# Macaron encoder layer on one Trainium2 core: inputs transposed by numpy, first blocks on undivided inputs, twelve blocks begun, a hand-set order of the end

## The chip, the cores and the metric

The kernel runs on one core of a Trainium2 chip. The core has five engines that each work through their own instructions in order: PE (matrix products into PSUM), DVE (VectorE), ACT (ScalarE), POOL (GpSimd) and SP (here it only issues DMAs). The metric is the device time of one execution in microseconds (us), lower is better; a program is run several times and the median counts. A profile is the record of one more execution.

## The reference, cut to what matters

Two independent token streams, x_prompt and x_sample, 512 tokens x 1024 channels each, float32, go through one layer and a last norm:

```
rms_norm(x, g) = x * rsqrt(mean(x*x, axis=-1) + 1e-6) * g
swiglu(x)      = (silu(x @ w_gate) * (x @ w_up)) @ w_down      # 1024 -> 2816 -> 1024
x = x + 0.5 * swiglu(rms_norm(x, ffn1_norm))                   # FFN1
x = x + mix(rms_norm(x, mix_norm))                             # attention and mLSTM, side by side
x = x + 0.5 * swiglu(rms_norm(x, ffn2_norm))                   # FFN2
y = rms_norm(x, final_norm)
```

The mean in rms_norm goes over the channels of one token, so 1/rms is one number for each token; it can be multiplied into x before a matrix product or into the product's result.

## The kernel before, in words

**Numbers.** Every float32 operand of a product is split into a high part (ACT copies it to the rounded type) and a low part (DVE subtracts the high part). A product of 128 x 128 by 128 x 512 is then three PE instructions: high by high, high by low, low by high. `w_pair` (L241) splits weights, `put` (L227) right operands.

**An FFN's first half.** A scheme of seven products in place of eight works on gate and up weights, the lower and upper half of the 1024 channels, and the two streams at once. Its seven right operands `xc` are B11 and B21 (lower and upper half of stream 0), B22 (upper half of stream 1) and the sums and differences T1 to T4. For one block of 128 of the 2816 columns (22 blocks) each of the seven is 4 x 3 = 12 PE instructions. `gu_first` (L286) does B11 and B21, which need stream 0 and the gate weights alone; its results are v1 (after B11) and silu(g0) (after B21). `gu_rest` (L301) does the other five. A block can be *begun* ahead: `begin` (L395) does B11 and B21 and parks v1 and silu(g0) in DRAM (`kept`), from where `resume` loads them. `rest` (L404) then goes through the blocks in the order `ORDER` (L368): resumed and fresh ones take turns while there are resumed ones. Before, AHEAD = 7 blocks are begun in both FFNs, so ORDER is 0, 7, 1, 8, ... 6, 13, 14, ... 21. Weights come through four buffers `wr` of 512 KB and, split, four buffers `w8`.

**An FFN's second half.** `ffn_down` (L449) multiplies by w_down in 28 steps (four groups of blocks by seven products, L533), whose operands were written to DRAM (`rbuf`) and are loaded again (`rt`). `flush_` (L541) adds each result from PSUM into the residual streams `xs` and calls `done(s, h, b)` when the block of tokens b, half h of the channels, stream s is complete.

**Opening.** `load_x` (L1148) loads raw tokens, 128 tokens x 1024 channels at a time, 512 KB each. `norm_x` (L1188) takes their sums of squares on DVE (L1195), 1/rms with `rstd_cols` (L151: a first guess from the bits of the number and three Newton steps, 12 small DVE operations) and multiplies it into the rows (L1201 on ACT, L1203 on DVE). `turn` (L1152) turns them with PE transposes (L1155) so that channels lie on partitions, `first_x` (L1215) multiplies with the norm's weights `g1` and splits (L1218 on ACT, L1219 on DVE). `park_x` (L1223) writes stream 0 to DRAM (`xnbuf`); `sums_of` (L1244) loads it again for the sums T1 to T4. Seven blocks are begun in between. `g1` is gathered by a DMA on POOL's queue (L125).

**End.** `done2` (L1346) takes the squares of a finished 128 x 512 piece on ACT (L1160), multiplies with `final_norm` (L1349, on POOL or DVE), and when a pair of token blocks is complete calculates 1/rms, multiplies it in (L1361 DVE, L1363 ACT) and stores 128 tokens x 1024 channels, 512 KB (L1364, SP's queue).

**What sets the order.** A list scheduler of the framework orders the instructions of each engine by readiness and priority. `shifted` moves a priority, `pin` (`keep_in_program_order`) keeps marked instructions in the order of the program. Nearly all DMAs are issued on SP's queue, in order. PSUM has pools of 3 (`MM`), 1 (`PO`), 2 (`PS`) and 2 (`PT`) banks.

Of the kernel before, what the change touches and what calls it, by code (L numbers as in the profile page):

```python
# [16 lines left out]
P = 128  # L17
# [9 lines left out]
def encoder(ctx, tc, I, outs):  # L27
# [97 lines left out]
    nc.gpsimd.dma_start(g1, I["ffn1_norm"][0].rearrange("(k p) -> p k", p=P))  # L125
# [25 lines left out]
    def rstd_cols(v, width, n):  # L151


        def t_(dt=F32):
            w = max(width, 4)
            return spool.tile([P, w], dt, tag=f"rs{w}", bufs=5, name=nm("rs"))[:, 0:width]
        V = nc.vector
        a = t_()
        V.tensor_scalar(a, v, 1.0 / n, EPS, op0=ALU.mult, op1=ALU.add)
        b = t_(I32)  # L160
        V.tensor_scalar(b, a.bitcast(I32), 1, None, op0=ALU.logical_shift_right)
        y_ = t_(I32)
        V.tensor_scalar(y_, b, -1.0, 1597463007.0, op0=ALU.mult, op1=ALU.add)
        y = y_.bitcast(F32)
        for _ in range(3):
            t = t_()
            V.scalar_tensor_tensor(t, y, -0.5, y, op0=ALU.mult, op1=ALU.mult)
            V.tensor_tensor(t, t, a, op=ALU.mult)
            r = t_()
            V.scalar_tensor_tensor(r, t, 1.5, y, op0=ALU.add, op1=ALU.mult)  # L170
            y = r
        return y

    def col_sums(acc, bs=(0, 1, 2, 3)):
# [4 lines left out]
        nc.vector.tensor_reduce(c, p[:, bs[0] * P:(bs[-1] + 1) * P].rearrange("p (b d) -> p b d", d=P), axis=AX.X,  # L179
                                op=ALU.add)  # L180
        return c
# [184 lines left out]
    AHEAD = 7  # L366

    ORDER = [j for p in zip(range(AHEAD), range(AHEAD, NF)) for j in p] + list(range(2 * AHEAD, NF))  # L368

    class Up:  # L370


        def __init__(self, xc, wg, wu, rb):
            self.xc, self.rb = xc, rb
            self.v = wg, wu
# [13 lines left out]
            r.junk = [r.o.rows[1][:, i] for i in range(2)]  # L389
            r.lone, r.last = lone, fa  # L390
# [13 lines left out]
        def rest(self, raw, at=None, hook=None):  # L404
            ring = self.ring
# [43 lines left out]
    def ffn_down(wd, rb, ring, tail, xres, done, at_step, hook):  # L449
# [19 lines left out]
        def load_raw(fp, i):  # L469
# [3 lines left out]
            fb = ORDER[2 * fp + i]  # L473
# [67 lines left out]
        def flush_(i, d, p):  # L541
# [3 lines left out]
            if last and m == T1:  # L545
                acc = xs[1][:, DH + d]
            if i < 7 and m in (B11, T2_, T1):
                nc.scalar.activation(acc, p, AF.Copy, scale=0.5)
            else:
                V_.scalar_tensor_tensor(acc, p, 0.5, acc, op0=ALU.mult, op1=ALU.add)  # L550
# [13 lines left out]
            elif m == T1:  # L564
                done(1, 1, d)
# [575 lines left out]
    raws = [A([P, 4, D], F32, "raw") for _ in range(2)]  # L1141
    xc = [None] * 7
    up = Up(xc, I["ffn1_w_gate"], I["ffn1_w_up"], rbuf[0])
    xins = [I[n][0] for n in ("x_prompt", "x_sample")]

    kept = [[dpool.tile([P, S], F32, name=f"kept{j}_{i}") for i in range(2)] for j in range(AHEAD)]

    def load_x(s):  # L1148
        for b in range(4):
            nc.sync.dma_start(raws[s][:, b, :], xins[s][b * P:(b + 1) * P, :])  # L1150

    def turn(s, k, banks):  # L1152
        p = banks[k % len(banks)]()
        for b in range(4):
            nc.tensor.transpose(p[:, b * P:(b + 1) * P], raws[s][:, b, k * P:(k + 1) * P], ident)  # L1155
        return p
# [31 lines left out]
    def norm_x(s):  # L1188

        sq = [spool.tile([P, 4], F32, tag="cs4", bufs=4, name=nm("cs4")) for _ in range(2)]  # L1190
        junk = up.ring.junk
        for b in range(4):
            for i in range(2):
                x_ = raws[s][:, b, i * S:(i + 1) * S]
                pin(V_.scalar_tensor_tensor(junk[i], x_, 1.0, x_, op0=ALU.mult, op1=ALU.mult,  # L1195
                                            accum_out=sq[i][:, b:b + 1]))
        pin(V_.tensor_tensor(sq[0], sq[0], sq[1], op=ALU.add))
        rs = rstd_cols(sq[0], 4, D)
        for b in range(4):
            if b % 2:  # L1200
                pin(nc.scalar.activation(raws[s][:, b, :], raws[s][:, b, :], AF.Copy, scale=rs[:, b:b + 1]))  # L1201
            else:
                pin(V_.tensor_scalar(raws[s][:, b, :], raws[s][:, b, :], rs[:, b:b + 1], None, op0=ALU.mult))  # L1203

    load_x(0)
    raw0 = up.fetch(0, (0,))
    load_x(1)
    raw1 = [up.fetch(j, (0,))[0] for j in (1, 2)]
    norm_x(0)
    W = [gu_left_a(raw0[0], pin)]  # L1210
    xc[B11], xc[B21] = xc_tile(), xc_tile()
    every = [PS, PT, PS, PT, MM, MM, PO]
    ps0 = {}

    def first_x(k):  # L1215
        t, kk, g = xc[B11 if k < HK_ else B21], k % HK_, g1[:, k:k + 1]
        p = ps0[k] = turn(0, k, every)
        nc.scalar.activation(t[:, 0, kk, :], p, AF.Copy, scale=g)  # L1218
        V_.scalar_tensor_tensor(t[:, 1, kk, :], p, g, f(t[:, 0, kk, :]), op0=ALU.mult, op1=ALU.subtract)  # L1219

    parked = []

    def park_x(k):  # L1223
        if k % 2 == 0:
            parked.append(up.ring.x())
        nc.scalar.activation(parked[-1][:, k % 2], ps0.pop(k), AF.Copy, scale=g1[:, k:k + 1])
        if k % 2:
            nc.sync.dma_start(xnbuf[:, k - 1:k + 1, :], parked[-1])

    for k in range(KD - 1):  # L1230
        first_x(k)
    park_x(0)
    first_x(KD - 1)
    W.append(gu_left_a(raw1[0], pin))
    up.begin(0, W[0])
    for k in range(1, KD):
        park_x(k)
    up.begin(1, W[1])
    norm_x(1)
    W.append(gu_left_a(raw1[1], pin))  # L1240
    raw0 += up.fetch(0, (1,))
    for i in (T2_, T1, T3, B22, T4):
        xc[i] = xc_tile()
# [10 lines left out]
    for k in (0, 2):  # L1254
        W.append(up.left(3 + k))
        sums_of(k, lambda kk, bank: turn(1, kk, [bank]), g1)
        W.append(up.left(4 + k))
        if k == 0:
            up.begin(2, W[2])
    for j in (3, 4, 5, 6):  # L1260
        up.begin(j, W[j])

# [5 lines left out]
    def done1(s, h, b):  # L1268
# [53 lines left out]
    up = Up(xc, I["ffn2_w_gate"], I["ffn2_w_up"], rbuf[1])  # L1322
# [23 lines left out]
    def done2(s, h, b):  # L1346
        x_ = xs[s][:, h * 4 + b, :]
        square(x_, ssq3[s][:, h, b:b + 1])
        (V_ if (s, h) == (1, 0) else G_).tensor_tensor(x_, x_, fn[h], op=ALU.mult)  # L1349
        if s == 0 and h == 1 and b == 3:  # L1350
            n = slice(0, 4)
        elif s == 1 and h == 0 and b % 2:
            n = slice(b - 1, b + 1)
        else:
            return
        r = row_scale(ssq3[s], n)
        for i in range(n.start, n.stop):
            v = xs[s].rearrange("p (h b) c -> p h b c", h=2)[:, :, i, :]
            r_ = r[:, i - n.start:i - n.start + 1]
            if s and i == 3:  # L1360
# [71 lines left out]
```

## Time and profile before

| | us |
|---|---|
| median of 3 runs (lowest, highest) | 2118.5 (2116.89, 2118.99) |
| the profiled execution | 2116.6 |
| its span (first to last record) | 2114.8 |
| PE busy in it | 2068.3 |
| first product of the FFN starts | 20.33 |
| first product of FFN1's second half starts | 450.10 |
| last product of the kernel starts (9 instructions, 2.20 us) | 2098.16 |

Times in the profile count from the start of the span. In a row of the timeline the columns are start, duration, engine, line, operation, what is written and read, shape, how many (x), and in brackets how long the engine had been idle before and what ended that. L12 is line 12 of the kernel that the row belongs to. Matmul durations overlap, so the distance from one start to the next is the time that one takes.

### The profile page before, as it was taken

What the parts mean: (1) busy time and instruction counts of PE and PEld (TensorE: products, weight loads), DVE (VectorE), ACT (ScalarE), POOL (GpSimd) and SP (SyncE); (2) the same over time, 40 slices, a digit from 0 to 9 for tenths busy, and PEclk for the clock granted to TensorE, in tenths of its full rate; (3) what the DMA queues carried; (4) which work ended last, traced back from release to release, by engine and by line L of the source; (5) the groups of instructions that cost most, each with busy time, mean ns of one, the idle gap of its engine ahead of it and who ended that gap; (6) DMA issues with size and microseconds to landing.
All of it is one profiled execution on the core that took longest, in us unless ns stands there. A gap on an engine that the chain in (4) does not pass through costs nothing.

```text
span 2114.8 us, 26230 instructions
## 1 busy us (share of the span) xinstructions
PE 2068.3 (98%) x9472; PEld 1692.4 (80%) x9472; DVE 1558.7 (74%) x2583; ACT 940.2 (44%) x1565; POOL 103.2 (5%) x110
## 2 busy tenths in 40 slices
PE   6999999999999999999999999999999999999997
PEld 5888888888888777878887787788888888888885
DVE  7888787776796896574649855754887877786696
ACT  6443443442225566463436555544544434343223
POOL 1000000001000110000101101010000000000002
PEclk9999999999999999999999999999999999999999
DMA  7464653489764222232341222354546545379763
GB/s 268 151 223 166 209 179 140 148 325 379 266 229 140 76 75 77 82 119 83 111 160 59 72 97 72 130 164 163 171 163 205 198 160 179 130 277 396 264 212 123
DMA packets 137425, 361.76 MB, mean 171 GB/s; under 512 B 13296, under 2 KB 13312, under 8 KB 136272
## 3 DMA queue, kind: packets, MB, share of 16 engines
q1 hardware_dynamic: 136704, 358.83, 48.6%
q0 software_dynamic: 592, 1.27, 0.2%
q8 instruction: 74, 1.21, 0.2%
q14 instruction: 55, 0.45, 0.1%
HBM read 255.15 MB, written 104.89 MB: 170 GB/s over the span
## 4 chain that ended last, share of the span: by engine, by line
PE 86%; DVE 7%; ACT 3%; DMA 2%; issue 1%; SPq 0%; POOL 0%; DVEq 0%; ACTq 0%; POOLq 0%
PE pss L283 17%; PE mm L686 14%; PE pst L283 11%; PE mm L283 10%; PE mm L533 7%; PE mm L670 4%; PE pst L533 4%; PE pss L533 4%; PE mm L1115 3%; PE pso L533 2%; PE pso L942 2%; PE pso L670 1%; PE pso L1071 1%; PE pss L914 1%; PE pss L1022 1%; PE pso L1115 1%
## 5 line engine op out<-in xcount | busy, mean ns | idle before, releaser
L283 PE MATMUL pss<-xc,w 128*128 128x512 f32 x1584 | 379.1, 389 | 0.0
L283 PEld LDWEIGHTS pss<-xc,w 128*128 128x128 f32 x1584 | 297.2, 188 | 62.0 <-DVE t L313 0.2
L686 PE MATMUL mm<-xh,w 128*128 128x512 f32 x896 | 294.1, 397 | 0.0
L283 PE MATMUL mm<-xc,w 128*128 128x512 f32 x1056 | 254.7, 391 | 2.9 <-ACT f L292 2.2
L242 ACT ACTIVATE w<-wr 128x1024 fp32r<-128x1024 f32 x132 | 139.7, 1060 | 235.3 <-PE pst L283 142.0
L283 PEld LDWEIGHTS mm<-xc,w 128*128 128x128 f32 x1056 | 196.7, 188 | 47.8 <-ACT f L292 6.3
L205 DVE TENSOR_TENSOR w<-wr,w 128x1024 fp32r<-128x1024 f32 (+1 forms) x112 | 136.6, 1221 | 114.1 <-ACT w L204 108.9
L243 DVE TENSOR_TENSOR w<-wr,w 128x1024 fp32r<-128x1024 f32 x132 | 161.1, 1222 | 80.2 <-ACT w L242 79.9
L686 PEld LDWEIGHTS mm<-xh,w 128*128 128x128 f32 x896 | 167.8, 189 | 32.4
L533 PE MATMUL mm<-w,rt 128*128 128x512 f32 x792 | 185.6, 389 | 0.9 <-DMA rt<-rbuf 0.9
L686 PE MATMUL mm<-xl,w 128*128 128x512 f32 x448 | 177.5, 396 | 0.0
L533 PEld LDWEIGHTS mm<-w,rt 128*128 128x128 f32 x792 | 148.4, 188 | 32.2 <-DMA rt<-rbuf 1.5
L204 ACT ACTIVATE w<-wr 128x1024 fp32r<-128x1024 f32 (+1 forms) x112 | 114.6, 1030 | 113.5 <-PE pso L1115 35.0
L283 PE MATMUL pst<-xc,w 128*128 128x512 f32 x528 | 127.1, 389 | 0.0
L283 PE MATMUL pst<-xc,f 128*128 128x512 f32 x528 | 127.0, 389 | 0.0
L283 PEld LDWEIGHTS pst<-xc,w 128*128 128x128 f32 x528 | 99.0, 188 | 20.8 <-ACT t L316 0.3
L283 PEld LDWEIGHTS pst<-xc,f 128*128 128x128 f32 x528 | 99.1, 188 | 20.6
L590 ACT ACTIVATE w<-t 128x512 fp32r<-128x512 f32 x82 | 51.6, 632 | 121.8 <-PE pst L533 63.6
L590 ACT ACTIVATE w<-wr 128x512 fp32r<-128x512 f32 x72 | 44.6, 631 | 129.8 <-PE pso L533 65.7
L686 PEld LDWEIGHTS mm<-xl,w 128*128 128x128 f32 x448 | 84.6, 189 | 16.2
L533 PE MATMUL pss<-w,rt 128*128 128x512 f32 x396 | 95.2, 390 | 1.3 <-ACT w L590 1.3
L533 PE MATMUL pst<-w,rt 128*128 128x512 f32 x396 | 94.3, 389 | 0.0
(323 smaller groups left out, 3497.8 us busy)
## 6 DMA issues: line engine op xcount, KB each, us to landing
rt<-rbuf SPq DMA_DIRECT2D x154, 512.0 KB, 6.2
rbuf<-t SPq DMA_DIRECT2D x72, 512.0 KB, 3.2
wr<-in_ffn_w_gate_dram SPq DMA_DIRECT2D x56, 512.0 KB, 4.2
wr<-in_w_in_cols_dram SPq DMA_DIRECT2D x56, 512.0 KB, 3.5
wr<-in_ffn_w_up_dram SPq DMA_DIRECT2D x44, 512.0 KB, 3.5
rbuf<-f SPq DMA_DIRECT2D x30, 512.0 KB, 3.2
rbuf<-tab SPq DMA_DIRECT2D x30, 512.0 KB, 3.6
wr<-in_ffn_w_down_dram SPq DMA_DIRECT2D x48, 256.0 KB, 7.6
```

Source lines behind the costliest of these rows:

```text
L204: pin(nc.scalar.activation(hi, raw, AF.Copy))
L205: pin(lo_eng.tensor_tensor(lo, raw, f(hi), op=ALU.subtract))
L242: pin(nc.scalar.activation(t[:, 0], src, AF.Copy))
L243: pin(V_.tensor_tensor(t[:, 1], src, f(t[:, 0]), op=ALU.subtract))
L283: nc.tensor.matmul(p, a[:, k, :], xt[:, b, k, :], start=(first and k == 0 and i == 0), stop=(k == HK_ - 1 and i == 2), skip_group_check=True)
L533: nc.tensor.matmul(p, r[:, b, d * P:(d + 1) * P], u[:, a, :], start=(first and q == 0 and k == 0), stop=(q == len(us) - 1 and k == 2), ski ...
L590: nc.scalar.activation(hi, src, AF.Copy)
L670: nc.tensor.matmul(p[b][:, :N], a[:, k, bs], w_[:, kl, :], start=(k == 0 and i == 0), stop=(k == KD - 1 and i == 2))
L686: nc.tensor.matmul(p, a[:, k, :], b, start=(k == 0 and i == 0), stop=(k == n - 1 and i == 2))
L914: nc.tensor.matmul(p, qT[:, h, b * P:(b + 1) * P], kv[:, hk * 2 + j, :], start=(j == 0), stop=(j == 1))
L942: nc.tensor.matmul(po, Vst[:, kv_, hk, :], w, start=(kv_ == 0 and i == 0), stop=(kv_ == 3 and i == 1))
L1115: nc.tensor.matmul(p[b], a[:, k, bs], w_[:, k - k0, :], start=(k == 0 and i == 0), stop=(k == KD - 1 and i == 2))
```

## The change

- numpy, ahead of the launch, transposes both inputs to channels on partitions (`x_prompt_t`, `x_sample_t`) and lays `ffn1_norm` out as 128 x 8; `g1` is loaded on SP's queue. `turn`, `norm_x`, `first_x` and `park_x` with their 64 PE transposes go.
- The first six blocks are begun on stream 0 times `g1` without 1/rms. The squares go to ACT (128 x 1024 at a time), their sums to DVE, the sum over partitions and the spreading of 1/rms along the tokens to PE transposes (`col_sums`, `bcast_psum`, 16 in all); `raw_end` multiplies 1/rms (R) into v1 and g0 on DVE before the Silu.
- Both streams are then multiplied by `g1` and R in place (`normed`), split anew, and blocks 6 to 11 begun on them: 12 blocks in FFN1, 7 still in FFN2. With 12, ORDER is 0, 12, 1, 13, ... 9, 21, 10, 11. The sums T1 to T4 are made on chip from 128 x 2048 operands.
- 1/rms is one Newton step and one of higher order: 11 small DVE operations for 12, everywhere.
- The end: `ends2` takes over the last product's results. Products with `final_norm` go to `e16` and `e5`, the mean square of half a row with eps is kept in `half_ms`, 1/rms of a pair starts from one fused operation (`last_scale`), the last piece is taken from PSUM in two halves of 256, stores of stream 1 are 256 KB each and two of them are issued by ACT. Stream 0's scaling and stores are spread between stream 1's squares on ACT.

The core of the diff:

```diff
-    nc.gpsimd.dma_start(g1, I["ffn1_norm"][0].rearrange("(k p) -> p k", p=P))
+    nc.sync.dma_start(g1, I["ffn1_norm"])
...
-        for _ in range(3):
-            t = t_()
-            V.scalar_tensor_tensor(t, y, -0.5, y, op0=ALU.mult, op1=ALU.mult)
-            V.tensor_tensor(t, t, a, op=ALU.mult)
-            r = t_()
-            V.scalar_tensor_tensor(r, t, 1.5, y, op0=ALU.add, op1=ALU.mult)
-            y = r
-        return y
+        t = t_()
+        pin(V.scalar_tensor_tensor(t, y, -0.5, y, op0=ALU.mult, op1=ALU.mult))
+        pin(V.tensor_tensor(t, t, a, op=ALU.mult))
+        pin(V.scalar_tensor_tensor(t, t, 1.5, y, op0=ALU.add, op1=ALU.mult))
+        y, t, p, q = t, y, b.bitcast(F32), t_()
+        pin(V.tensor_tensor(t, y, y, op=ALU.mult))
+        pin(V.tensor_tensor(t, t, a, op=ALU.mult))
+        pin(V.tensor_scalar(p, t, 0.375, -1.25, op0=ALU.mult, op1=ALU.add))
+        pin(V.tensor_tensor(p, p, t, op=ALU.mult))
+        pin(V.scalar_tensor_tensor(q, p, 1.875, y, op0=ALU.add, op1=ALU.mult))
+        return q
...
-    AHEAD = 7
+    RAW, AHEAD = 6, (12, 7)
+    def order_of(ahead):
+        return [j for p in zip(range(ahead), range(ahead, NF)) for j in p] + (
+            list(range(2 * ahead, NF)) or list(range(NF - ahead, ahead)))
...
+    load_half(0, 0)
+    load_x(0, 0, 1)
+    load_x(0, 1, 2)
+    load_x(0, 2, 4)
+    load_half(1, 0)
+    load_half(0, 1)
+    load_x(0, 4, 6)
+    load_x(0, 6, 8)
+    load_half(1, 1)
+    raw2 = up.fetch(2, (0,))
+    for k in range(0, KD, 2):
+        load_x(1, k, k + 2)
...
+    def split_x(k):
+        t, kk, g, x = xr[k // HK_], k % HK_, g1[:, k:k + 1], x_t[0][:, k, :]
+        nc.scalar.activation(t[:, 0, kk, :], x, AF.Copy, scale=g)
+        V_.scalar_tensor_tensor(t[:, 1, kk, :], x, g, f(t[:, 0, kk, :]), op0=ALU.mult, op1=ALU.subtract)
+    def squares(s, i):
+        sq = stat[0] if i == 0 else stat[1 + i % 2]
+        pin(nc.scalar.activation(sq, x_t[s][:, 2 * i:2 * i + 2, :], AF.Square))
+        if i:
+            pin(V_.tensor_tensor(stat[0], stat[0], sq, op=ALU.add))
+    def norm(s):
+        acc = stat[0][:, 0]
+        pin(V_.tensor_tensor(acc, acc, stat[0][:, 1], op=ALU.add))
+        r = rstd_cols(col_sums(acc, pin=pin), 4, D, pin)
+        pin(nc.scalar.activation(R[s], bcast_psum(r), AF.Copy))
+    def normed(s):
+        for k in range(KD):
+            x = x_t[s][:, k, :]
+            pin(V_.scalar_tensor_tensor(x, x, g1[:, k:k + 1], R[s], op0=ALU.mult, op1=ALU.mult))
...
+    def raw_end(j):
+        X, v1 = begun.pop(j)
+        g0 = gate_rows()
+        pin(V_.tensor_tensor(v1, v1, R[0], op=ALU.mult))
+        pin(V_.tensor_tensor(g0, X, R[0], op=ALU.mult))
+        pin(nc.scalar.activation(g0, g0, AF.Silu))
+        up.kept[j] = kept[j]
+        for t, d in zip((v1, g0), kept[j]):
+            nc.sync.dma_start(d, t)
...
+    first_left(0, 0)
+    for k in range(HK_):
+        split_x(k)
+    raw_lower(0)
+    first_left(1, 0)
+    first_left(0, 1)
+    for k in range(HK_, KD):
+        split_x(k)
+        if k % 2:
+            squares(0, k // 2 - 2)
+    raw_lower(1)
+    raw_upper(0)
+    first_left(1, 1)
+    raw_upper(1)
+    squares(0, 2)
+    squares(0, 3)
+    norm(0)
+    raw_next(2)
+    raw_end(0)
+    raw_end(1)
+    raw_next(3)
+    raw_end(2)
+    normed(0)
+    raw_next(4)
+    raw_end(3)
     xc[B11], xc[B21] = xc_tile(), xc_tile()
+    for i, t in zip((B11, B21), halves(0)):
+        put_all(xc[i], t)
+    raw_next(5)
+    raw_end(4)
+    for i in range(4):
+        squares(1, i)
+    norm(1)
+    raw_end(5)
+    ahead(6)
+    normed(1)
+    ahead(7)
...
+    def last_scale(b0):
+        a = rs_tile(2)
+        sq, hm = ssq3[1][:, 0, b0:b0 + 2], half_ms[0][:, b0:b0 + 2]
+        pin(V_.scalar_tensor_tensor(a, sq, 1.0 / D, hm, op0=ALU.mult, op1=ALU.add))
+        return rstd_of(a, 2, pin)
...
+        for c in (slice(0, H), slice(H, S)):
+            pin(V_.scalar_tensor_tensor(acc[:, c], p[:, c], 0.5, acc[:, c], op0=ALU.mult, op1=ALU.add))
+            if c.start == 0:
+                pin(nc.scalar.activation(junk[:, c], acc[:, c], AF.Square, accum_out=ssq))
+        hm = half_ms[0][:, 3:4]
+        more = spool.tile([P, 4], F32, tag="cs4", bufs=4, name=nm("more"))[:, 0:1]
+        pin(V_.scalar_tensor_tensor(junk[:, H:], acc[:, H:], 1.0, acc[:, H:], op0=ALU.mult, op1=ALU.mult, accum_out=more))
+        pin(V_.scalar_tensor_tensor(hm, more, 1.0 / D, hm, op0=ALU.mult, op1=ALU.add))
+        for h in range(2):
+            on_act(1, h, first_r[0][:, 1:2])
+        r = last_scale(2)
+        pin(V_.scalar_tensor_tensor(acc, acc, r[:, 1:2], fn[0], op0=ALU.mult, op1=ALU.mult))
+        on_act(3, 1, r[:, 1:2], nc.scalar)
+        pin(store(1, 3, 0, acc))
+        pin(V_.tensor_scalar(pre1[:, 2], pre1[:, 2], r[:, 0:1], None, op0=ALU.mult))
+        pin(store(1, 2, 1, pre1[:, 2]))
+        on_act(2, 0, r[:, 0:1], nc.scalar)
```

The program of the changed kernel has the same order of instructions as before on every engine from FFN1's second half to the last step of FFN2.

More of the change, by code (lines that the diff above doesn't have):

```diff
@@ L388, in __init__ @@
             r.k = Ring([fb[:, 0], fb[:, 1]])
-            r.junk = [r.o.rows[1][:, i] for i in range(2)]
-            r.lone, r.last = lone, fa
+            r.lone, r.last, r.order = lone, fa, self.order
         def fetch(self, j, which=(0, 1)):
@@ L447, in encoder, with ffn_down @@
     n_steps = len(DOWN) * len(CHUNKS)
-    def ffn_down(wd, rb, ring, tail, xres, done, at_step, hook):
+    def ffn_down(wd, rb, ring, tail, xres, done, at_step, hook, ends=None):
         n = n_steps
@@ L546, in flush_ @@
                 acc = xs[1][:, DH + d]
+            if last and m == B22 and ends:
+                ends(d, p, acc, e16, e5)
+                return
             if i < 7 and m in (B11, T2_, T1):
@@ L1221, in encoder @@
[L1221 to L1238, printed above, removed]
```

212 lines of the change are left out of this document (125 added, 87 removed).

## The prediction

> **What bounds the kernel now.** I read the page's busy shares first, then the span cut into stretches (columns: start:end, length, busy time and records of PE, PEld, DVE, ACT and POOL, granted PE clock, DMA share, GB/s), then PE's waits and the timeline of the two ends.
>
> ```profile
> span 2114.8 us, 26230 instructions
> ...
> PE 2068.3 (98%) x9472; PEld 1692.4 (80%) x9472; DVE 1558.7 (74%) x2583; ACT 940.2 (44%) x1565; POOL 103.2 (5%) x110
> ...
> 0.00:20.30 20.30, 8.28 (x43) 7.75 (x44) 11.21 (x36) 6.88 (x10) 5.55 (x12) 0.75 0.92 309
> 20.30:74.90 54.60, 49.85 (x232) 39.46 (x231) 50.55 (x76) 41.67 (x59) 0.00 (x0) 1.00 0.70 237
> 74.90:102.10 27.20, 27.20 (x122) 22.52 (x121) 20.11 (x28) 9.17 (x13) 0.00 (x0) 1.00 0.34 107
> 102.10:450.10 348.00, 348.00 (x1537) 288.13 (x1536) 277.79 (x354) 141.41 (x183) 0.00 (x0) 1.00 0.53 184
> ...
> 450.10 2.20 PE L533 MATMUL mm<-w,rt 128*128 128x512 f32 x9
> ...
> 2100.40:2114.80 14.40, 0.00 (x0) 0.00 (x0) 7.34 (x32) 4.78 (x7) 0.00 (x0) 0.64 0.38 146
> ```
>
> PE is the bound: from 74.9 to 450.1 it never stops. 348.00 us over 1537 records is 0.2264 us for a product; I use 0.2267, twelve in 2.72 us. So a change outside the products can win only from the 20.3 us ahead of the first one, the stalls up to 74.9, and the 14.4 us behind the last. My ruler for the opening: counted along the order of the instructions, 312 products are done at 102.1. Back to back they take 312 x 0.2267 = 70.7 us, so the opening loses 31.4 us.
>
> ```profile
> PE pss L1155 <- DVE raw L1203: 13.4, 2, 11.0
> ...
> 10.98 0.69 DVE L1195 SCALAR_TENSOR_TENSOR tab<-raw 128x512 f32<-128x512 f32 x1 [1.35 <-DMA raw<-in_x_prompt_dram]
> ...
> 16.38 0.42 PE L1155 MATMUL pst<-ident,raw 128*128 128x128 f32 x1
> 16.59 0.42 PE L1155 MATMUL pss<-ident,raw 128*128 128x128 f32 x1
> ...
> 20.33 2.55 PE L283 MATMUL mm<-xc,w 128*128 128x512 f32 x10
> ...
> 36.84 0.33 PE L1155 MATMUL pss<-ident,raw 128*128 128x128 f32 x1 [2.41 <-DVE raw L1203]
> 37.00 0.27 PE L1155 MATMUL pst<-ident,raw 128*128 128x128 f32 x1
> 37.11 0.27 PE L1155 MATMUL pss<-ident,raw 128*128 128x128 f32 x1
> ```
>
> The first product waits for a chain: the last block of raw rows is read at 10.98, then come squares, 1/rms, scaling, transposes and splitting, until 20.33. The clock shows too: after the 11.0 us without work the transposes start 0.21 us apart (16.38 to 16.59), after 2.41 us 0.11 apart (37.00 to 37.11). A wait of about 11 us costs PE half its speed for a while, one of 2.4 us doesn't.
>
> **The opening: PE starts early, DVE then sets the pace.** DVE and ACT work in strict order, so I follow the built order with the spacing of back-to-back rows.
>
> ```profile
> 0.00:3.75 3.75, 2.71 (x12) 2.71 (x13) 0.18 (x2) 1.49 (x2) 2.62 (x8) 1.00 0.50 140
> 3.75:6.00 2.25, 1.07 (x6) 0.78 (x4) 1.31 (x4) 0.00 (x0) 2.22 (x4) 1.00 1.00 382
> 6.00:10.50 4.50, 0.00 (x0) 0.00 (x0) 2.62 (x8) 0.00 (x0) 0.00 (x0) 0.79 1.02 222
> ...
> 13.13 0.16 DVE L167 SCALAR_TENSOR_TENSOR rs<-rs 128x4 f32<-128x4 f32 x1
> 13.33 0.16 DVE L168 TENSOR_TENSOR rs<-rs,rs 128x4 f32<-128x4 f32 x1
> ...
> 18.52 0.68 ACT L1218 ACTIVATE xc<-pst,g 128x512 fp32r<-128x512 f32 x1
> 19.09 0.68 ACT L1218 ACTIVATE xc<-pss,g 128x512 fp32r<-128x512 f32 x1
> ...
> 19.22 0.75 DVE L1219 SCALAR_TENSOR_TENSOR xc<-pss,g,xc 128x512 fp32r<-128x512 f32 x1
> 19.88 0.74 DVE L1219 SCALAR_TENSOR_TENSOR xc<-pst,g,xc 128x512 fp32r<-128x512 f32 x1
> ...
> 58.76 1.22 DVE L230 TENSOR_TENSOR xc<-t,xc 128x1024 fp32r<-128x1024 f32 x1
> 59.89 1.22 DVE L236 TENSOR_TENSOR t<-t,t 128x1024 f32<-128x1024 f32 x1
> ...
> 78.64 0.68 DVE L266 TENSOR_TENSOR wr<-wr 128x512 f32<-128x512 f32 x1
> 79.24 0.68 DVE L322 TENSOR_TENSOR t<-t 128x512 f32<-128x512 f32 x1
> ```
>
> - First product. ACT's order takes three half weight tiles (block 0 lower, block 1 lower, block 0 upper) before the first slice of x, so it waits for the seventh DMA on SP: 1.84 MB. The rates above give 3.75 x 140 + 2.25 x 382 = 1.39 MB at 6.00 and the other 0.45 at 222 GB/s by 8.0; with something for the landing I take 8.3. Bounds are 7 us (382 GB/s from 3.75 on) and 10.98 us (where the fourth 512 KB of raw landed). Two ACT steps of 0.57 and the start make the first product 9.7 us, bounds 8.4 and 12.4. The eight slices of x then leave DVE 0.66 apart, the last at about 15.0.
> - DVE from 15.0 to the low half of block 11's weights (`w_pair`, L243 here, L250 in the changed kernel), which the twelfth begun block needs: 34 ops of 128x512 at 0.60 = 20.4, 22 of 128x1024 at 1.13 = 24.9, 7 of 128x2048, 22 small ones at 0.20 = 4.4. The trace has no 128x2048: two more steps of (1.13 - 0.60) = 0.53 for each 512 columns give 2.2, bounds 1.6 (1.13 + 0.53: one step only) and 2.4 (four times 0.60); 7 x 2.2 = 15.4. Sum 65.1. Waits within it: 1.5 for the ACT squares, 2.0 and 1.0 for the two broadcasts of 1/rms through PE and ACT, about 0.4 elsewhere: 4.9. Block 11's weights are ready at 15.0 + 65.1 + 4.9 = 85.0.
> - PE beside it. Six undivided blocks (144 products) are done by about 43. Block 6 needs the normalized operand, whose low half leaves DVE at 47.5. 124 products at 0.2267 and the transposes bring PE to 76.5; there it waits 8.5 us for block 11's weights. Of the 312 products 268 are then done. From 85.0: 44 x 0.2267 = 10.0, 1.1 of waiting for the next low half (that of a T1 weight, L603 in the changed kernel, L591 here), 0.1 of start: 96.2.
> - The clock after those 8.5 us: the rows have full speed after 2.41 us and half after 11.0. 8.5 is nearer to the second, so I take half speed: the ten products before the L603 wait take 4.5 instead of 2.3, of which that wait hides 1.1: +1.1, so 97.3. Bounds 96.2 and 99.5 (half speed for 3.4 us, nothing hidden).
>
> 312 products done at 97.3 instead of 102.1: **the opening gains 4.8 us** (26.6 lost instead of 31.4), although the first product comes 10.6 earlier.
>
> The Trainium skill, "TensorE: Matmul & The Clock Gate", section "Part 1: The HAM clock gate", says that PE drops to half rate after an idle window of about 3.4 us and needs as long a busy one to come back. That speaks against this change: it puts a long wait where PE was warm. By the rule the sum is the same 97.3, without it 96.2; both of the rows above agree with it.
>
> Costed at nothing: 48 PE instructions fewer (64 transposes gone, 16 added, 0.11 each), since DVE sets the pace; if it doesn't, they are worth 5 us more, inside rival A. Five more kept pairs (5 x 2 x 256 KB out and back, 5.2 MB, at 382 GB/s 14 us of DMA) lie in the stretch to 450.1 whose DMA share is 0.53; the parked x and its loads go. On SP the weight loads queue behind those stores, which wait for a Silu; four weight buffers cover that by my count, and a miss shows as a DMA wait of ACT. The norm weights move from POOL to SP and lead its queue (32 bytes a partition). The order of resumed and fresh blocks ends on two resumed ones in a row; its operands are ready about 1 us ahead; without that cover it costs up to 1. Each 1/rms of the middle has 11 small ops instead of 12, 0.2 us where PE waits for it; I leave it in the range.
>
> **The end.**
>
> ```profile
> 2098.16 2.20 PE L533 MATMUL pso<-w,rt 128*128 128x512 f32 x9
> ...
> 2101.37 0.16 DVE L159 TENSOR_SCALAR rs<-rsum 128x2 f32<-128x2 f32 x1
> ...
> 2103.11 0.68 DVE L550 SCALAR_TENSOR_TENSOR xs<-pso,xs 128x512 f32<-128x512 f32 x1
> 2103.82 0.63 ACT L1160 ACTIVATE f<-xs 128x512 f32<-128x512 f32 x1 [1.56 <-DVE xs L550]
> ...
> 2107.62 0.16 DVE L170 SCALAR_TENSOR_TENSOR rs<-rs,rs 128x2 f32<-128x2 f32 x1
> 2107.88 1.15 ACT L1363 ACTIVATE xs<-xs,rs 128x1024 f32<-128x1024 f32 x1 [0.95 <-DVE rs L170]
> ...
> 2106.95 3.30 SPq L1364 DMA_DIRECT2D out_dram<-xs  x3
> ...
> 2111.00:2113.00 2.00, 0.00 (x0) 0.00 (x0) 0.00 (x0) 0.00 (x0) 0.00 (x0) 0.50 0.98 377
> ```
>
> The last product ends at 2100.36, but DVE reads it only at 2103.11, behind the 1/rms of the first pair (from 2101.37). Last issue 2110.25 (2106.95 + 3.30), data at 377 GB/s until 2113, span end 2114.8. After, in the same frame: the first pair's 1/rms needs only two products and lies at 2099.0 to 2101.05; the third product is taken in by 2101.7, the last in halves (0.35 each) by 2103.0, its square sums by 2104.0, 11 small ops to 2106.2; then 0.6 on DVE beside 0.6 on ACT, once more each to 2107.9. The last issue ends at 2108.3, 2.0 earlier, and what follows is 256 KB instead of 512 KB: 0.6 at 377 GB/s. **The end gains 2.6 us.** Not in the trace is an issue on ACT's queue: bounds are 0.32 and 2.28 us, SP's issues.
>
> ```profile
> 28.66 0.32 SPq L399 DMA_DIRECT2D kept<-f  x1
> ...
> 32.22 2.28 SPq L1246 DMA_DIRECT2D t<-xnbuf  x1
> ```
>
> I take 0.32, nearest for an empty queue; at 2.28 the scale queued behind it on ACT comes 2.0 later and 0.6 is left. So 0.6 to 3.5 (the whole second half's scaling hidden), and no loss, since the last product is no longer behind a 1/rms.
>
> **Sum.** 2116.6 (this execution; 2114.8 span and 1.8 around it) - 4.8 - 2.6 = 2109.2. The runs shown have their median at 2118.5, 1.9 higher, which would make it 2111.1. I say **2110.0**.
>
> **Rivals.**
>
> ```profile
> L243 DVE TENSOR_TENSOR w<-wr,w 128x1024 fp32r<-128x1024 f32 x132 | 161.1, 1222 | 80.2 <-ACT w L242 79.9
> ```
>
> - A, DVE isn't the pace: the scheduler's slack or shorter wide ops let block 11 through, and PE runs on from 76.5. For it: only 4.9 of the 85 are waits. Against it: 65.1 us of DVE work that the first four steps show. It gives the 8.5 and the 1.1 of the clock and the 1.1 of waiting behind it: 10.7 more, 2098.5, by the median 2100.4.
> - B, the opening gains nothing (the change doesn't do what it says): loads as late as raw's 10.98 (+2.7) and rows at their duration instead of their spacing (0.68 for 0.60 and 1.22 for 1.13 over 56 ops: up to +4.7). From +4.8 on only the end is left: 2114.0, by the median 2115.9.
> - C, slower: each low half on DVE waits for ACT's high half, as row L243 does (80.2 us over 132: 0.61 each). The opening has some 20 such pairs in the chain from 15.0: +12.2 on top, so -4.8 becomes +7.4; with the end 2121.4, by the median 2123.3. It decides from (4.8 + 2.6)/20 = 0.37 us a pair. Against it: ACT had less to do than DVE in that stretch of before (41.67 of 54.60 us, DVE 50.55), and along the built order its high halves are ready ahead of DVE but for the 4.9 us above.
>
> **Chances.** Forecast (2106 to 2113) 0.54, A 0.11, B 0.21, C 0.14. The range 2100 to 2118 holds the forecast, B and half of A, about 8 in 10. A measurement here tells 0.2%, 4.2 us, from no change: forecast and A are faster by more (0.65), B within it (0.21), C slower (0.14).
>
> **What would show it.** Right: first product near 9.7 us; a PE idle time near 77 to 85 that DVE's L250 ends; the first ffn_down product near 445.3 instead of 450.1; span end some 11.8 us behind the last product instead of 14.4. Wrong: no such idle time (A); DVE waiting for ACT w again and again before 85 (C); first product past 12 (B); a PE wait for kept or rt in between, or a last issue held up on ACT's queue.

## The result, and the profile after

The changed kernel takes 2114.93 us (median of 20 runs, 2111.65 to 2116.53), the kernel before 2117.57 (20 runs). The ratio of the runs is 0.9983, with a 95% interval of 0.9977 to 0.9989: 3.6 us faster (2.3 to 4.9), within the 0.2% that I had called no change. (The two medians lie 2.6 us apart; the ratio is not their quotient. Gains below are from the ratios.) The time lies in the stated range (2100 to 2118); I had forecast 2110.0, and what came is the time that rival B gives (2114.0 to 2115.9).

The span after, cut where the one before was cut (first product, 74.9, 102.1, start of FFN1's second half, end of the last product):

```profile
0.00:12.20 12.20, 3.67 (x16) 3.48 (x16) 2.06 (x5) 3.97 (x7) 4.21 (x11) 0.82 0.76 218
12.20:74.90 62.70, 61.27 (x257) 48.00 (x258) 56.87 (x84) 41.47 (x53) 0.00 (x0) 0.95 0.66 239
74.90:102.10 27.20, 18.85 (x74) 14.59 (x73) 26.18 (x25) 12.74 (x15) 0.00 (x0) 0.87 0.31 107
102.10:449.80 347.70, 347.70 (x1535) 287.96 (x1534) 289.55 (x376) 139.72 (x182) 0.00 (x0) 1.00 0.58 204
...
2101.60:2113.10 11.50, 0.02 (x1) 0.00 (x0) 5.65 (x21) 5.01 (x10) 0.00 (x0) 0.59 0.49 182
```

The first product comes 8 us earlier (12.27 instead of 20.33) and the end behind the last product is 11.5 instead of 14.4 us. But from 74.9 to 102.1, where PE had worked without a pause, it now stands still for 8.35 us while DVE is busy for 26.18 of 27.20. PE's two long waits up to 110 (us in total, times, longest):

```profile
PE mm L290 <- DVE w L250: 8.3, 1, 8.3
PE mm L290 <- ACT xc L1229: 7.6, 1, 7.6
```

I counted the same products in both traces. After minus before, at the start of: the 313th product -0.45 us, the first of FFN1's second half -0.22, the products at 500 us -2.2, the last product +1.26; what follows the last product -2.97. So there are two gains (1.9 us at the start of the second half, 3.0 at the end), next to nothing from the opening, and a loss of 3.4 us between 700 us and the last product, against this one trace of before.

One sentence ahead of the prediction is not right: the order of instructions from FFN1's second half on is not the same. In the attention part of the mix PE, ACT and DVE have some operations in another order (of PE's 7544 instructions of that part, 148 places, all between 712 and 1483 us, hold one of another shape). The shorter 1/rms has moved them: with the old arithmetic put back (e1), the order of all three in the mix is that of before again, and with the shorter one put into the kernel before (e2), PE's is that of the changed kernel.

### The profile page after: what moved, and what is told of

Its sections match the earlier page's. It is cut to its first block, busy times and chain, and to the rows that moved or that the text cites. A ratio compares the mean times of both kernels' runs of the same rounds, so it can differ in the third digit from the quotient of the medians.

```text
span 2113.1 us, 26149 instructions
## 1 busy us (share of the span) xinstructions
PE 2067.0 (98%) x9424; PEld 1689.1 (80%) x9424; DVE 1575.7 (75%) x2568; ACT 939.7 (44%) x1559; POOL 100.6 (5%) x105
## 3 DMA queue, kind: packets, MB, share of 16 engines
q0 software_dynamic: 560, 1.26, 0.2%
## 5 line engine op out<-in xcount | busy, mean ns | idle before, releaser
L249 ACT ACTIVATE w<-wr 128x1024 fp32r<-128x1024 f32 (+1 forms) x134 | 139.8, 1047 | 254.0 <-PE pst L290 134.3
L250 DVE TENSOR_TENSOR w<-wr,w 128x1024 fp32r<-128x1024 f32 (+1 forms) x134 | 161.4, 1206 | 82.2 <-ACT w L249 81.5
L212 DVE TENSOR_TENSOR w<-wr,w 128x1024 fp32r<-128x1024 f32 (+1 forms) x112 | 135.4, 1210 | 116.2 <-ACT w L211 111.3
L211 ACT ACTIVATE w<-wr 128x1024 fp32r<-128x1024 f32 (+1 forms) x112 | 114.6, 1030 | 109.8 <-PE pso L1127 35.0
```

The source lines that it names most:

```text
L211: pin(nc.scalar.activation(hi, raw, AF.Copy))
L212: pin(lo_eng.tensor_tensor(lo, raw, f(hi), op=ALU.subtract))
L249: pin(nc.scalar.activation(t[:, 0], src, AF.Copy))
L250: pin(V_.tensor_tensor(t[:, 1], src, f(t[:, 0]), op=ALU.subtract))
```

## The experiments

Two theories on the opening: **D**, DVE's chain sets the time of everything up to the T2 weights; **P**, PE or a load sets it. On the 3.7 us that the trace loses in the attention (700 to 770): **R**, the new order of instructions there costs it; **T**, PE only comes earlier and waits there; **N** (added later), it is spread between executions.

### The parts alone (e1 to e4, 11 runs each, before at 2117.77)

e1 puts the old arithmetic of 1/rms into the changed kernel:

```diff
-        t = t_()
-        pin(V.scalar_tensor_tensor(t, y, -0.5, y, op0=ALU.mult, op1=ALU.mult))
...
-        y, t, p, q = t, y, b.bitcast(F32), t_()
...
-        pin(V.scalar_tensor_tensor(q, p, 1.875, y, op0=ALU.add, op1=ALU.mult))
-        return q
+        for _ in range(3):
+            t = t_()
+            pin(V.scalar_tensor_tensor(t, y, -0.5, y, op0=ALU.mult, op1=ALU.mult))
+            pin(V.tensor_tensor(t, t, a, op=ALU.mult))
+            r = t_()
+            pin(V.scalar_tensor_tensor(r, t, 1.5, y, op0=ALU.add, op1=ALU.mult))
+            y = r
+        return y
```

> The changed kernel with the old arithmetic of 1/rms back (three Newton steps, 12 small DVE operations); opening and end as changed. Theory R (the shorter 1/rms made the list scheduler interleave ACT and DVE differently in the attention part of the mix, where the trace of the changed kernel loses 3.1 us between 712 and 764): the order in the mix is again that of before, those losses go, 0.2 us for each longer 1/rms on the path comes back (0.4 to 0.8): 4.0 us faster than the kernel before, about 1.4 faster than the changed kernel; PE's waits for L933/L929 (ACT and DVE in the attention) fall back to those of before. Rival T (PE simply comes to the mix 2 us earlier and DVE or ACT set the end there): no gain, 2.0 us faster than before, waits as in the changed kernel.

Measured: 2113.28, ratio 0.9981 (0.9972 to 0.9989): 4.0 us faster than before (2.3 to 5.9). That is R's number, and T's 2.0 lies outside the interval. But the changed kernel itself is 3.6 faster and not the 2.6 that R counted from. The intervals of the two lie over each other, so R's 1.4 us between them is not seen. e2 is the kernel before with the new `rstd_of`, so the same lines the other way round:

```diff
-        for _ in range(3):
...
+        y, t, p, q = t, y, b.bitcast(F32), t_()
...
+        return q
```

> The kernel before with the new 1/rms alone (11 small operations). Theory R: slower than before by 1.4 us (2 us lost in the attention part of the mix, 0.6 saved at the waits for 1/rms); the trace loses 2 to 3 us against before between 712 and 764. Rival T: faster by 0.4 to 0.6, nothing lost there, since PE does not come to the mix earlier.

Measured: 2117.98, ratio 1.0002 (0.9993 to 1.0011). Its trace loses 3.8 us between 700 and 770, as R says, and has 1.6 of them back by 870. The time doesn't decide: its interval, 1.5 us faster to 2.3 slower, holds R's 1.4 slower and T's 0.5 faster. e3 is the changed opening with the old end and the old 1/rms. Against the changed kernel:

```diff
-    def done2(s, h, b, spare=None):
+    def done2(s, h, b):
...
-    def last_scale(b0):
...
```

e4 is the kernel before with the changed end (`ends2`, `last_scale`, `done2`) and the old 1/rms. Against the changed kernel:

```diff
-    RAW, AHEAD = 6, (12, 7)
+    AHEAD = 7
...
+    raws = [A([P, 4, D], F32, "raw") for _ in range(2)]
```

> The changed opening alone (transposed inputs, six undivided blocks, 12 begun), with the old 1/rms and the old end. From the trace of the changed kernel: 0.1 to 0.3 us gained at the first products behind the opening, 1.7 more at the start of FFN1's second half (the DMA waits there go). Theory R: 1.8 to 2.0 us faster than before. Rival T: the mix takes that back, no difference (0 to 0.3 faster).

> The changed end alone, with the old opening and the old 1/rms. The trace of the changed kernel has 2.9 us less behind the last product. Expected 2.5 us faster than before (2.9 less two 1/rms that are one operation longer, 0.2 each), the whole of it behind the last product. Rival (an end that only looks shorter, since the last product itself comes later by the new order of ACT and DVE): under 1 us.

Measured: e3 2115.29, ratio 0.9990 (0.9981 to 0.9999), 2.1 us faster (0.2 to 4.0; R had 1.8 to 2.0, T up to 0.3); e4 2115.59, ratio 0.9989 (0.9981 to 0.9998), 2.3 us faster (0.4 to 4.0; 2.5 expected). Opening and end alone add up to 4.4, where both together with the old 1/rms bring 4.0 (e1). In e3's trace the opening itself is no gain (at 450 us it is 0.9 later than before); it makes up 1.95 us between 450 and 500. That PE never waits there is seen in the stretches of before and of e3:

```profile
400.00:420.00 20.00, 20.00 (x90) 16.56 (x89) 13.43 (x17) 8.03 (x10) 0.00 (x0) 1.00 0.23 79
...
460.00:480.00 20.00, 19.57 (x87) 15.88 (x86) 11.72 (x18) 8.40 (x15) 2.60 (x4) 1.00 1.04 401
480.00:500.00 20.00, 19.07 (x85) 15.39 (x84) 10.86 (x17) 5.83 (x10) 4.26 (x8) 1.00 1.03 378
```

```profile
400.00:420.00 20.00, 20.00 (x90) 16.53 (x89) 16.16 (x21) 7.66 (x11) 0.00 (x0) 1.00 0.91 324
...
460.00:480.00 20.00, 20.00 (x90) 16.57 (x89) 11.95 (x20) 8.24 (x15) 2.59 (x4) 1.00 1.05 391
480.00:500.00 20.00, 20.00 (x90) 16.53 (x90) 14.29 (x21) 6.78 (x12) 5.78 (x8) 1.00 1.03 387
```

With 12 blocks begun the order closes on resumed ones, and the transfers run at 324 instead of 79 GB/s already from 400 to 420. That the operands of the second half are then in time, and that this is why the DMA and ACT stalls at 460 to 500 (0.43 + 0.93 us of PE) are gone, is read from the traces; no run changes the order alone. All ten traces with 12 begun blocks gain 1.6 to 2.0 us there on the first trace of before. Of the others with 7, e4 gains nothing on it, the second trace of before 0.3, but e2 1.3. So the order is worth some 0.7 to 2.0 us, and the 1.95 is its upper end.

### The mix (e13: the kernel before, a second trace)

e13 has no edit: it is the kernel before once more.

> The kernel before once more, for a second trace of it. Theory N (the 3.7 us that the changed kernel loses against before between 700 and 770, in the attention part of the mix, are the spread of that part from one execution to the next, since e4_end_alone with before's instruction order there lost 2.4): this trace differs from the first one of before by 1.5 to 4 us there. Rival R (the order of ACT and DVE there, changed by the shorter 1/rms, costs it): under 0.7.

The stretch 700 to 770 in the first trace of before, in its second, in e4 (the same order of instructions as before up to the end of FFN2) and in the changed kernel:

```profile
700.00:770.00 70.00, 67.69 (x343) 53.29 (x342) 66.94 (x140) 42.69 (x88) 10.63 (x7) 1.00 0.23 72
```

```profile
700.00:770.00 70.00, 65.99 (x329) 51.49 (x329) 67.57 (x135) 41.76 (x86) 9.82 (x7) 1.00 0.24 72
```

```profile
700.00:770.00 70.00, 65.58 (x330) 51.32 (x330) 67.73 (x134) 41.32 (x84) 9.40 (x7) 1.00 0.23 72
```

```profile
700.00:770.00 70.00, 65.17 (x321) 50.60 (x320) 65.94 (x131) 39.93 (x80) 12.84 (x8) 1.00 0.24 74
```

The second trace is 2.0 us later than the first across this stretch, e4 2.4, as N says: the one trace of before that I had read was a lucky one there. At the last product the changed kernel is 1.26 us behind the first trace of before and 0.13 behind the second. All the traces together say the same. From the products at 710 us to those at 870, the nine with the short 1/rms, so with the new order, lose 0.9 to 3.5 us on the first trace of before (2.1 in the mean), and the four others with the old order (e1, e3, e4, e13) lose 1.2 to 2.3 (1.8 in the mean). What the new order costs in the attention is a few tenths at most by these means, less than the spread, and is not shown.

### The opening: is it DVE? (e5, e6, e7)

From here on most kernels were timed once or a few times, and the mix alone varies by 2 to 3 us from one execution to the next, so I go by the counted products of the opening and not by the run's time.

e6 takes work from DVE:

```diff
-            pin(V_.scalar_tensor_tensor(x, x, g1[:, k:k + 1], R[s], op0=ALU.mult, op1=ALU.mult))
+            pin(V_.scalar_tensor_tensor(x, x, g1[:, k:k + 1], R[0], op0=ALU.mult, op1=ALU.mult))
...
-    for i in range(4):
-        squares(1, i)
-    norm(1)
```

> The changed kernel without stream 1's own sums of squares and 1/rms in the opening (stream 1 is multiplied by stream 0's 1/rms: that part of the computation is left out). It takes from DVE three sums of 128x1024 (1.13 each), two 128x512 (0.6), 11 small operations (0.2), 6.8 us in all, and about 2 us of waiting for PE and ACT between them; from PE only 8 transposes. Theory D: the low half of block 11's weights comes 7 to 9 us earlier, the PE wait of 8.3 us shrinks to 0 to 1.5, and the 312th product comes 6.5 to 8.5 earlier. Rival P (PE is held by loads or by ACT at that place): the wait stays over 5 us.

Measured: 2107.71 in one run (before 2119.48 on that chip); the 313th product at 95.46 instead of 101.49, 6.0 us earlier (D had 6.5 to 8.5), first of the second half 6.2 earlier. PE's waits:

```profile
PE mm L290 <- ACT f L299: 2.2, 3, 0.8
...
PE mm L290 <- DVE w L250: 1.1, 1, 1.1
```

The 8.3 us have become 1.1. That is D in kind, and a little short of it in size. e6 also takes four squares from ACT, but in the changed kernel ACT is busy for only 12.74 of the 27.20 us around that wait. e7 leaves all the work and moves block 11 ahead in the queue:

```diff
     put_all(xc[T1], x0l)
     ahead(8)
+    ahead(9)
+    ahead(10)
+    ahead(11)
...
-    ahead(9)
...
-    ahead(10)
...
-        if m == T2_:
-            ahead(11)
```

> The changed kernel with the weights of blocks 9, 10 and 11 asked for ahead of the sums T3, T2 and T4, so that block 11's split stands earlier in DVE's queue; the same work in another order. Theory D (the whole of DVE's work up to the T2 weights counts): the PE wait of 8.3 us ahead of block 11 goes or moves, and one of the same size comes at the first product with T2 or T1; the 312th product within 1 us of the changed kernel's 101.5. Rival B11 (what costs the 8.3 us is that one late split): 6 to 8 us earlier.

Measured: 313th product at 99.37, 2.1 us earlier (one run: 2109.47, before 2119.48). The wait has moved: 

```profile
PE pss L290 <- ACT w L249: 3.6, 1, 3.6
PE mm L290 <- ACT w L249: 1.7, 1, 1.7
```

It now stands at the first T2 product and behind it. The 289th product is 10.5 us earlier than in the changed kernel (85.5 instead of 96.1), and 8.4 of that are lost again up to the 313th. So the late split of block 11 alone is not the cause, and neither theory has the 2.1. It is ACT's high half of the T2 weights that ends both waits. ACT works in order, and it had stood idle at a copy out of PSUM ahead of them:

```profile
86.23 0.60 ACT L305 ACTIVATE f<-mm 128x512 f32<-128x512 f32 x1 [3.17 <-PE mm L290]
```

What stands ahead of the T2 weights on DVE and ACT comes up again with e12. e5 was to show the late start of DVE's chain:

```diff
-        w_pair(W[j]["t"][:, :, a], half(first_w[j], a))
+        w_pair(W[j]["t"][:, :, a], half(first_w[j], a), pin)
...
-        nc.scalar.activation(t[:, 0, kk, :], x, AF.Copy, scale=g)
-        V_.scalar_tensor_tensor(t[:, 1, kk, :], x, g, f(t[:, 0, kk, :]), op0=ALU.mult, op1=ALU.subtract)
+        pin(nc.scalar.activation(t[:, 0, kk, :], x, AF.Copy, scale=g))
+        pin(V_.scalar_tensor_tensor(t[:, 1, kk, :], x, g, f(t[:, 0, kk, :]), op0=ALU.mult, op1=ALU.subtract))
```

> The changed kernel with one thing more: the splits of the first two weight tiles and of the eight slices of x are kept in program order, which is that of the loads, so ACT and DVE take the slices 0 to 3 of x while the two half weight tiles that the changed kernel waits for (ACT idle for 5.55 us until 10.35) are still under way. Theory D (DVE sets the pace from the first split to the low half of the T2 weights, 96.2 to 99.7 in the changed kernel): first product at about 6.5 us instead of 12.3, the last slice of x leaves DVE at about 14.5 instead of 17.6, and every later DVE step, block 11's weights (88.4) and the 312th product (about 101.5) come 2.5 to 3.5 us earlier; the PE wait of 8.3 us stays. Rival P (PE or a load sets the pace): the wait ahead of the first product goes, and the wait at block 11 grows by as much; under 1 us at the 312th product.

Measured: first product at 5.79, and the 313th at 106.27, 4.8 us later (run 2117.52, before 2119.48). Neither theory had that. ACT's timeline:

```profile
9.86 1.33 ACT L1229 ACTIVATE xc<-xt,g 128x512 fp32r<-128x512 f32 x2 [1.28 <-DMA xt<-in_x_prompt_t_dram]
13.96 0.60 ACT L1254 ACTIVATE t<-mm 128x512 f32<-128x512 f32 x1 [2.76 <-PE mm L290]
14.45 1.14 ACT L249 ACTIVATE w<-wr 128x512 fp32r<-128x512 f32 x2
```

With a product finished early, the scheduler put its copy out of PSUM ahead of the next two weight tiles; ACT waited for PE until 13.96, and the last slice of x left DVE at 19.8 instead of 17.6. A start of PE 6.5 us earlier was worth less than nothing because it held up ACT, and with it DVE.

### Repairs (e10, e11, e9, e12)

e10 is e5 with `raw_lower(0)` moved behind the last slice of x. Against e5:

```diff
-    raw_lower(0)
...
+    raw_lower(0)
     raw_lower(1)
```

> As e5_arrival_order, with the first product's copy out of PSUM (L1254) moved behind the last slice of x in the program, since in e5 ACT stood 2.76 us at that copy until 13.96 and the two weight tiles behind it came at 14.5 instead of 10.4. Theory D (DVE's chain sets the pace): last slice of x off DVE at 14 to 15.5 (17.6 in the changed kernel, 19.8 in e5), 312th product 2 to 3.5 us earlier than the changed kernel's 101.5, so at 98 to 99.5; the first product of FFN1's second half at 446.5 to 448. Rival P (not DVE's start, but a wait in the middle, such as ACT's copies of finished products, sets it): within 1 us of 101.5 or later.

Measured: 313th product at 99.18, 2.3 earlier (run 2111.64, before 2117.26). As D expected in size, but the last slice left DVE at 17.2, only 0.4 earlier: the loads gave no more. The rest came from ACT's squares, for which DVE had waited 2.44 us in the changed kernel.

e11 puts e7's edit into e10. Against e10:

```diff
+    ahead(9)
+    ahead(10)
+    ahead(11)
...
-        if m == T2_:
-            ahead(11)
```

> e10 and e7 together: the first splits in the order of the loads and the weights of blocks 9 to 11 ahead of the sums. e7 alone brought the 312th product 2.1 us earlier, e10 should bring 2 to 3.5. Theory D: 4 to 5.5 us together at the 312th product (96 to 97.5), first product of FFN1's second half at 444.5 to 446, the run 2110 to 2111.5 where the changed kernel has 2114.9 (before 2117.6). Rival: the two gains are the same wait and do not add: 2 to 3.5 us.

Measured: 2111.79 (9 runs; before 2117.26), ratio 0.9974 (0.9963 to 0.9985), 5.5 us faster than before. But the 313th product is at 100.37, 1.1 earlier than in the changed kernel: the two gains don't add, as the rival says (it had 2 to 3.5). As in e7, PE waits for ACT's high half of the T2 weights (3.6 and 2.6 us). e9 is e5 (without the moved copy) with the sums of squares on PE:

```diff
-        if i:
-            pin(V_.tensor_tensor(stat[0], stat[0], sq, op=ALU.add))
+        if i % 2:
+            for b in range(4):
+                for n, (u, q) in enumerate((u, q) for u in (i - 1, i) for q in range(2)):
+                    nc.tensor.matmul(col[s][:, 2 * i - 2 + b:2 * i - 1 + b], stat[u % 3][:, q, b * P:(b + 1) * P],
+                                     ones[:, 0:1], start=(n == 0), stop=(n == 3), skip_group_check=True)
```

> The changed kernel with the arrival order of the first splits and with the sums of the squares taken on PE: 64 products of 128 channels x 128 tokens with a column of ones (one column wide) replace DVE's four sums and the reduction of each stream (4.6 us of DVE a stream). Theory D: DVE's chain loses 3 us at the start and 9 us in between, PE gains 3 to 7 us of small products; then PE is the bound again: 312th product at 89 to 93 instead of 101.5, 8 to 12 us faster than the changed kernel, 2103 to 2107 beside 2114.9. Rival: the time returns as waits behind the opening (DVE has its work of the first ordinary block still ahead), and under half of it is left at the first product of FFN1's second half (449.9).

Measured: 2129.48 (5 runs; before 2119.48), ratio 1.0045 (1.0031 to 1.0059); 313th product at 120.6, 19 us later than in the changed kernel, of which e5's order alone brings 4.8. PE's narrow products from 5 to 110 as a group, two bursts of them in the timeline with what follows each, and three stretches:

```profile
L1241 PE MATMUL pst<-ones,t 128*128 128x1 f32 x128 | 18.7, 278 | 0.0
```

```profile
62.94 3.63 PE L1241 MATMUL pst<-ones,t 128*128 128x1 f32 x32
66.43 0.72 PE L290 MATMUL mm<-xc,w 128*128 128x512 f32 x2
...
69.66 5.97 PE L1241 MATMUL pst<-ones,t 128*128 128x1 f32 x28
75.48 7.60 PE L290 MATMUL mm<-xc,w 128*128 128x512 f32 x21
```

```profile
20.00:40.00 20.00, 20.00 (x101) 17.60 (x100) 6.21 (x11) 7.68 (x10) 0.00 (x0) 0.74 0.34 116
40.00:60.00 20.00, 18.54 (x81) 14.18 (x80) 15.86 (x29) 10.95 (x14) 0.00 (x0) 1.00 0.53 190
60.00:83.00 23.00, 22.91 (x105) 20.25 (x106) 9.10 (x18) 7.12 (x10) 0.00 (x0) 0.70 0.42 139
```

My 3 to 7 us stood on 64 instructions of 0.05 to 0.11 us. A product one column wide is two instructions, so there are 128. From start to start they take 0.11 us in the first burst (62.94 to 66.43, 32 of them) and 0.21 in the second (69.66 to 75.48, 28 of them), where the granted clock is 0.50 (69.7 to 75.2). In the two stretches that hold them it is 0.74 and 0.70 in the mean, for the wide products too (0.35 us each in the row at 75.48), although PE is busy all the time. Both 1/rms then come late, and DVE runs dry (6.21 of 20.00 busy). e12 is e11 with a part given to POOL:

```diff
+            if s and k >= HK_:
+                G_.tensor_tensor(x, x, R[s], op=ALU.mult)
+                pin(nc.scalar.activation(x, x, AF.Copy, scale=g1[:, k:k + 1]))
+            else:
```

> e11 with four of the sixteen multiplications of x by 1/rms (upper half of stream 1) moved from DVE to POOL, which is idle there, and the multiplication by the norm's weights for these four to ACT. Theory D alone: 4 x 0.66 = 2.6 us less on DVE, 312th product 2 to 2.6 us earlier than in e11. Rival S (POOL and DVE slow each other: in the profile before, one 128x512 product on DVE took 1.30 instead of 0.69 us while POOL was multiplying): the DVE steps beside the four POOL steps stretch to 1.0 to 1.3 us and nothing is gained, or up to 3 us lost.

Measured: one run of 2105.94 (before 2117.26), the shortest time of all; 313th product at 93.7, 6.7 earlier than in e11 (D had 2 to 2.6). But not for the reason expected. DVE and POOL side by side:

```profile
62.23 6.86 DVE L1251 SCALAR_TENSOR_TENSOR xt<-xt,g,tab 128x512 f32<-128x512 f32 x4
```

```profile
61.87 6.67 POOL L1248 TENSOR_TENSOR xt<-xt,tab 128x512 f32<-128x512 f32 x4 [60.57 <-ACT tab L1242]
```

The four on DVE took 1.7 us each beside POOL's four, where eight take 5.38 alone: rival S, 1.5 us lost. Two things came with the edit that were not meant. POOL's four small gathers (`gain`, `gbias`, `hn`) slid from 1.4 us to 68.5, behind that work. The loads at the start, e11 and then e12:

```profile
4.00:6.00 2.00, 1.07 (x5) 0.78 (x4) 0.96 (x2) 1.35 (x2) 0.73 (x1) 1.00 0.85 190
```

```profile
4.00:6.00 2.00, 0.82 (x4) 0.53 (x3) 0.69 (x1) 1.34 (x2) 0.00 (x0) 1.00 0.91 323
```

The last slice of x leaves DVE at 15.1 instead of 17.2. The trace of before has the same gathers 1.4 us later, issued at 2.9 to 5.2, and there the loads go with 379 GB/s from 4 to 6 and fall to 236 and 198 from 6 to 10. That speaks for the gathers as the cause, but no run moves them alone. The second thing is that the T2 weights are split ahead of the last operands, e12 and then e11:

```profile
87.22 2.36 DVE L250 TENSOR_TENSOR w<-wr,w 128x1024 fp32r<-128x1024 f32 x2
```

```profile
96.42 3.49 DVE L250 TENSOR_TENSOR w<-wr,w 128x1024 fp32r<-128x1024 f32 x3
```

The counted products tell the two apart. The 289th starts at 86.9 in e12 and at 86.5 in e11, so nothing of the earlier loads is left by then. The whole 6.7 us come between it and the 313th, at the T2 products, although DVE ends its last split of the operands (L237) 0.7 us later than in e11 (97.2, 96.5). So the time follows the T2 weights, as D says, but how much stands ahead of them is a matter of order and not only of the amount of DVE's work. No run changes this order alone, and e12 was timed once only.

## Why the prediction was right or wrong, point by point

- **PE bound, two ends to win**: right. Between 102.1 and 449.8 PE still works without a pause.
- **First product** (9.7): 12.27. The mechanism was right, the landing was mis-sized: I took 8.3 us for the seventh load, from the mean rates of before, where its rows had 10.98 for the same kind of load. ACT's rows have it at 10.35, near the late end of my bounds, and it then had two half weight tiles to split and not one (0.6 us more):

```profile
10.35 1.26 ACT L249 ACTIVATE w<-wr 128x512 fp32r<-128x512 f32 x2 [5.55 <-DMA wr<-in_ffn_w_gate_dram]
11.51 5.00 ACT L1229 ACTIVATE xc<-xt,g 128x512 fp32r<-128x512 f32 x8
```

- **DVE from the last slice to block 11's weights** (70.0 with waits): 72.0, from 17.6 to 89.6.

```profile
20.68 3.89 DVE L1236 TENSOR_TENSOR t<-t,t 128x1024 f32<-128x1024 f32 x3 [2.44 <-ACT t L1234]
...
37.29 5.38 DVE L1247 SCALAR_TENSOR_TENSOR xt<-xt,g,t 128x512 f32<-128x512 f32 x8
...
72.69 4.58 DVE L1283 TENSOR_TENSOR xc<-xt,xc 128x2048 fp32r<-128x2048 f32 x2
...
88.40 1.22 DVE L250 TENSOR_TENSOR w<-wr,w 128x1024 fp32r<-128x1024 f32 x1
```

The 128x2048 op takes 2.2 us, as extrapolated (the second starts 2.2 after the first and the pair ends at 4.58). But 16 of the 34 steps of 128x512 are scalar_tensor_tensor at 0.66, not 0.60 (1.0 us), and the waits were 5.9 and not 4.9.
- **PE's wait and the clock**: right. 8.35 us (8.5), ended by L250, and behind it half speed: ten products in 4.0 us, then full.

```profile
89.68 4.20 PE L290 MATMUL mm<-xc,w 128*128 128x512 f32 x10 [8.35 <-DVE w L250]
93.71 1.08 PE L290 MATMUL pst<-xc,f 128*128 128x512 f32 x4
```

Behind the wait the 44 products took 11.8 us (12.3), since the second wait, at L603, didn't come.

So the step that failed is the size of the opening's gain: 4.8 forecast, 0.4 measured. 2.6 of what is missing is the start and 2.0 DVE's chain. That is rival B's mechanism in part (late loads, longer steps), with its sign (a first product past 12 us) and its result; C was not there (L250 waited 0.6 us for ACT up to 102). And I took the order in which DVE's work stands as given, where e7 and e12 move the 313th product by 2.1 and, with the start of e10, by 7.8 us.
- **Costed at nothing**: the new order of blocks. I asked only whether its last two resumed blocks could stall (up to 1 us lost). It goes with 0.7 to 2.0 us of gain at the start of the second half, where the transfers start earlier (e3); the cause is read from the traces.
- **The end** (2.6): 2.97, in every kernel with the new end and the short 1/rms between 2.96 and 2.98; 2.5 and 2.4 with the long one (e4, e1). The issues on ACT's queue took 0.40 and 0.34:

```profile
2107.84 0.40 ACTq L1443 DMA_DIRECT2D out_dram<-e  x1
...
2109.04 0.34 ACTq L1443 DMA_DIRECT2D out_dram<-e  x1
```

- **The sum**: -7.4 forecast; the quiet stretches of the trace give -0.2 (up to 450) - 1.9 - 3.0 = -5.1 against the first trace of before, and -3.9 with the 0.7 that the order gains on e2. The runs have -3.6 (-2.3 to -4.9). The rest is within what the mix varies by from one execution to the next. That the time lies in the range is not to the credit of the forecast: the range held rival B's outcome too, of the two gains that I had counted only the end came, and the order of the blocks, which I had not, made up for a part of the other. That was luck.

## What to carry to other kernels

When PE's first work is moved forward, the engine that feeds it can become the bound, as DVE did here: add up that engine's steps to the point where the old order had caught up, and the earlier start counts only as far as that sum allows. Then look at the order of these steps: what PE needs next should not stand behind what it needs later (e7, e12). Loads of the first microseconds should be priced by the latest landing that the trace has; small gathers on another queue are a suspect there, not tried by themselves. Before a difference of 2 to 3 us in one stretch is explained, take a second trace of the same program.

## What the runs showed of the hardware that I had not expected

- Float32 products one column wide are two instructions each, 0.11 us apart at full clock and 0.21 at half, and in the stretches that hold them PE's granted clock is 0.70 to 0.74 in the mean, with PE counted as busy for 42.91 of 43.00 us (e9).
- DVE and POOL on 128x512 float32 tensors at the same time: 1.7 us each, where DVE alone takes 0.66 (e12; POOL alone was not measured). Four of eight steps moved to POOL cost DVE 1.5 us more than they took off.
- Four gathers of 2 to 8 KB from POOL, issued at 1.4 to 4.7 us, go with 190 instead of 323 GB/s for the loads from 4 to 6 us (e11 against e12, which differ in more than this).
